# Attention's norm chains on ScalarE and GpSimd, and p's parts and the projection's first weight formed in the last slab in the values' buffers

## The chip, the cores and the metric

The kernel runs on one core of a Trainium2 chip. Its engines run side by side, each through its own list of instructions in order: TensorE (PE) multiplies matrices and transposes, VectorE (DVE), ScalarE (ACT) and GpSimd (POOL) work element by element, SyncE (SP) issues most transfers. What a program on one engine needs from another it waits for by semaphore. The metric is device time in microseconds (us) of one execution; runs of before took 1295.8 us in the median of three (1295.56 to 1299.09).

## What is computed

A trunk of two layers on one sequence of 512 tokens and 1024 features, in float32. Layer 0 mixes by a causal convolution, layer 1 by differential attention; each mixer is followed by a SwiGLU block and by a gated input embedding `p`. The change lies in layer 1, from attention to the gate:

```python
def diff_attention(x, w_qkv, q_g, k_g, ..., sub_g, w_o, rel_bias, lambda_init):
    q, k, v = jnp.split(x @ w_qkv, 3, axis=-1)          # 8 heads, two halves of 64 for q and k
    q = rms_norm(q.reshape(B, S, N_HEADS, 2, HEAD_DIM), q_g) * (HEAD_DIM ** -0.5)
    k = rms_norm(k.reshape(B, S, N_HEADS, 2, HEAD_DIM), k_g)
    ...
        logits = q_blk @ k + bias                        # causal, blocks of 128 queries
        probs = jax.nn.softmax(logits, axis=-1)
        w = probs[:, :, 0] - lam * probs[:, :, 1]        # the second half is taken off
        return w @ v
    o = rms_norm(o, sub_g) * (1.0 - lambda_init)         # per head, 128 features
    return o @ w_o

h = h + diff_attention(rms_norm(h, attn_norm_g), ...)
h = h + swiglu(rms_norm(h, ffn_norm_g), w_gate, w_up, w_down)
h = h + sigmoid(rms_norm(h, ple_norm_g) @ ple_w_gate) * (p @ ple_w_proj)
```

`rms_norm` divides by the root of the mean square plus an epsilon of 1e-6.

## The kernel before

**Tiling.** Features lie on the 128 partitions, tokens along the free axis: `h` is eight tiles of 128x512. Every product runs as three matmuls (`mm3`, lines 156 to 158), since each operand is held as a rounded high part and a remainder. `weight()` (line 136) makes the two parts of a 128x1024 block of weights: SP loads it into one of two raw buffers (`wraw`, line 145), ACT casts the high part (`whi`, line 149), DVE or POOL subtracts for the low part (`wlo`, line 151); `whi` and `wlo` have four buffers each. A raw buffer is free for the next load only once its low part is made.

**Order.** The program is written as one sequence; a scheduler then orders each engine's list by a simulated timeline, keeping dependencies. A tile is named by a tag with so many buffers, and a new tile of a tag waits until all readers of the old one in that buffer are done. So what the change moves is seen in the lists of the engines.

**Attention.** The loop over `QKV` (line 897) has six slabs of four weights: q and k of head pair 0, values of heads 0 to 3, pairs 1 and 2, values of heads 4 to 7, pair 3. Each slab runs over four blocks of 128 tokens (`tokens`, 24 matmuls a block). `values` leaves its two parts in the tiles B0 to B3 (heads 0 to 3) and B4 to B7. `unit` forms q and k of a pair: ACT copies and squares (lines 757, 760), DVE sums over 64 features (764) and adds the epsilon (235), POOL raises to the power -1/2 (237) and multiplies (767); `unit_end` transposes on PE (773) and writes the parts into the tiles C0 to C5 (two buffers each, so pair 3 takes pair 1's).

Between these matmuls stand the stages of the 32 pairs of head and query block: `stage_s` (logits 818 and 819 on PE, bias and minimum 821 and combining 830 on DVE, exponential 825 on ACT), `stage_t` (transposes 838, parts 840 and 841) and `stage_a` (product with the values 854 and 855, evacuation 861 and 862). After a head's last block `stage_a` normalises it: ACT squares all 512 columns (866), DVE sums (868), inverts the first softmax's sum (870), multiplies twice by it (871, 872) and adds the epsilon (235), POOL takes the power, DVE multiplies once more (874), POOL scales the head (876). `stage_o` transposes it (883) and splits it into the tiles A (180, 181).

**After the slabs.** `pfeatures` loads the two halves of p into raw buffers and splits them (lines 274, 275) into new tiles of the tags C0 and C1, whose next buffers are those of pair 2. `project` forms eight 128x512 products of p from two weights, with one step of the remaining attention stages before each. Then `linear` makes the attention's output product, eight outputs of 24 matmuls: the first two together, each head as it is ready, then one by one; `add_attn` adds each to `h` (951). PSUM has four accumulators of the tag `mm` for slabs, values, projections and outputs alike.

## Time and profile before

| | |
|---|---|
| median of three runs | 1295.8 us (1295.56 to 1299.09) |
| the profiled execution, its time | 1293.82 us |
| its span | 1292.0 us |
| instructions in the span | 15534 |

The profile is of one execution on the chip; times in it count from the start of the span, and the rest of that execution's time lies around it. A row of instructions names line, engine, operation, the tile written and those read, and the shape. Behind a bar stand busy time and the mean of one in nanoseconds. A table of windows gives for each stretch the busy time of each engine, its count of instructions, then the clock granted to PE and the share of the transfer engines. PE's matmuls are pipelined, so that one of 0.39 us in a row is followed by the next 0.23 us later.

### The profile page before, as it was taken

The page shows a single profiled execution, that of the slowest core. Times are in us where ns is not written, and L with a number is a line of the kernel's source. Part 1 is how long each engine was busy: PE and PEld are TensorE (multiplying, and loading weights), DVE is VectorE, ACT ScalarE, POOL GpSimd, SP SyncE. Part 2 cuts the span into 40 slices and gives each one's busy share as a digit, 9 for nine tenths or more (in the row PEclk, how much of TensorE's full clock was granted, in tenths as well). Part 3 has the DMA queues.
Part 4 walks back from the last instruction along what each step waited for, and adds up shares of the span by engine and source line. Part 5 has one row for each costly group of instructions (what it writes and reads, how often), then busy time and mean ns, then how long its engine had stood idle before and what let it go on. Part 6 is the DMA issues. An engine that isn't in the chain of part 4 may idle for free.

```text
span 1292.0 us, 15534 instructions
## 1 busy us (share of the span) xinstructions
PE 1269.5 (98%) x5960; PEld 1053.6 (82%) x5960; DVE 736.9 (57%) x1143; ACT 521.6 (40%) x826; POOL 236.8 (18%) x199
## 2 busy tenths in 40 slices
PE   9999999999999999999999997989999999999998
PEld 8888788888888888888888886878888888888887
DVE  4897866543344334457678988845443344334445
ACT  5742554332222223345566766634222233222332
POOL 1753432000000000042526534121000000000020
PEclk9999999999999999999999998999999999999999
DMA  7555223333333322233222223123333333332231
GB/s 273 192 177 181 80 76 104 98 98 98 98 98 99 97 86 95 82 117 98 88 90 74 74 66 83 57 76 103 99 98 94 89 97 96 98 98 90 90 115 66
DMA packets 46839, 131.98 MB, mean 102 GB/s; under 512 B 5379, under 2 KB 9987, under 8 KB 46764
## 3 DMA queue, kind: packets, MB, share of 16 engines
q1 hardware_dynamic: 44640, 127.55, 31.0%
q10 hardware_dynamic: 2124, 3.43, 1.0%
q8 instruction: 47, 0.77, 0.2%
q14 instruction: 28, 0.23, 0.1%
HBM read 126.75 MB, written 4.21 MB: 101 GB/s over the span
## 4 chain that ended last, share of the span: by engine, by line
PE 88%; DVE 6%; DMA 3%; issue 2%; ACT 1%; POOL 0%; SPq 0%; DVEq 0%; POOLq 0%; ACTq 0%
PE mm L156 28%; PE mm L157 27%; PE mm L158 27%; DVE sc L419 2%; DVE wlo L151 1%; PE tp L173 1%; PE mm L854 1%; DMA wraw<-in_wts 1%; DMA po<-big 1%; PE sc L818 1%; PE sc L368 1%; PE sc L819 1%; PE tp L838 1%; PE tp L773 0%; DMA h<-in_xT 0%
## 5 line engine op out<-in xcount | busy, mean ns | idle before, releaser
L149 ACT CAST whi<-wraw 128x1024 fp32r<-128x1024 f32 (+2 forms) x213 | 217.6, 1026 | 554.6 <-PE mm L158 364.1
L156 PE MATMUL mm<-A,wlo 128*128 128x512 f32 (+1 forms) x1096 | 427.9, 390 | 4.5 <-DVE wlo L151 3.0
L157 PE MATMUL mm<-A,whi 128*128 128x512 f32 (+1 forms) x1096 | 425.7, 389 | 0.0
L158 PE MATMUL mm<-A,whi 128*128 128x512 f32 (+1 forms) x1096 | 421.8, 389 | 0.0
L151 DVE TENSOR_TENSOR wlo<-wraw,whi 128x1024 fp32r<-128x1024 f32 (+2 forms) x209 | 259.4, 1245 | 84.8 <-ACT whi L149 84.7
L156 PEld LDWEIGHTS mm<-A,wlo 128*128 128x128 f32 x1096 | 206.0, 188 | 48.5 <-DVE wlo L151 3.5
L157 PEld LDWEIGHTS mm<-A,whi 128*128 128x128 f32 x1096 | 206.0, 188 | 42.8 <-issue 1.2
L158 PEld LDWEIGHTS mm<-A,whi 128*128 128x128 f32 x1096 | 205.4, 188 | 42.3 <-issue 0.5
L204 POOL TENSOR_TENSOR acc<-acc,wk 128x512 f32<-128x512 f32 x35 | 58.2, 1662 | 772.3 <-issue 660.1
L156 PE MATMUL mm<-B,wlo 128*128 128x512 f32 x352 | 137.8, 391 | 0.0
L157 PE MATMUL mm<-B,whi 128*128 128x512 f32 x352 | 137.4, 390 | 0.0
L158 PE MATMUL mm<-B,whi 128*128 128x512 f32 x352 | 137.4, 390 | 0.0
L635 DVE TENSOR_TENSOR h<-mm,h 128x512 f32<-128x512 f32 x48 | 33.0, 691 | 122.6 <-PE mm L158 122.5
L627 DVE TENSOR_TENSOR big<-mm,rb 128x512 f32<-128x512 f32 x44 | 30.4, 691 | 126.4 <-PE mm L158 126.4
L625 DVE TENSOR_TENSOR big<-mm,rb 128x512 f32<-128x512 f32 x44 | 30.4, 691 | 99.8 <-PE mm L158 93.0
L158 PEld LDWEIGHTS mm<-B,whi 128*128 128x128 f32 x352 | 66.1, 188 | 14.6
L157 PEld LDWEIGHTS mm<-B,whi 128*128 128x128 f32 x352 | 66.1, 188 | 14.3
L156 PEld LDWEIGHTS mm<-B,wlo 128*128 128x128 f32 x352 | 66.0, 188 | 14.2
L156 PE MATMUL mm<-whi,A 128*128 128x512 f32 x192 | 75.9, 396 | 0.0
L157 PE MATMUL mm<-whi,A 128*128 128x512 f32 x192 | 75.5, 393 | 0.0
L158 PE MATMUL mm<-wlo,A 128*128 128x512 f32 x192 | 74.7, 396 | 0.0
L237 POOL TENSOR_TENSOR r<-v,mhalf 128x8 f32<-128x8 f32 (+1 forms) x31 | 45.8, 1477 | 144.3 <-DVE v L235 135.8
(203 smaller groups left out, 1397.4 us busy)
## 6 DMA issues: line engine op xcount, KB each, us to landing
wraw<-in_wts SPq DMA_DIRECT2D x193, 512.0 KB, 3.5
wraw<-in_wts SPq DMA_DIRECT2D x16, 384.0 KB, 3.0
D<-in_diag SPq DMA_DIRECT2D x22, 256.0 KB, 4.3
C<-in_diag SPq DMA_DIRECT2D x16, 256.0 KB, 4.8
h<-in_xT SPq DMA_DIRECT2D x8, 256.0 KB, 5.4
bias<-scr ACTq DMA_DIRECT2D x8, 256.0 KB, 3.5
out_t<-h SPq DMA_DIRECT2D x7, 256.0 KB, 2.0
wraw<-in_wts SPq DMA_DIRECT2D x4, 256.0 KB, 5.0
```

The lines of the kernel that those rows point to most:

```text
L149: A.copy(hi[:, cut], raw[:, cut])
L151: eng.tensor_tensor(lo[:, cut], raw[:, cut], f(hi[:, cut]), ALU.subtract)
L156: T.matmul(acc, al, bh, start=first, stop=False)
L157: T.matmul(acc, ah, bh, start=False, stop=False)
L158: return T.matmul(acc, ah, bl, start=False, stop=last)
L173: r = T.matmul(t[:, cut], src[:, cut], ones, start=first and b == 0, stop=last and b == 3)
L204: self.last = self.eng.tensor_tensor(self.acc, self.acc, sq, ALU.add)
L237: last_pow[0] = G.tensor_tensor(r[:, :n], v[:, :n], mhalf[:, :n], ALU.pow)
L419: last_v_tap[0] = V.scalar_tensor_tensor(sum_, tap(j), wt(c, j), sum_, ALU.mult, ALU.add)
L625: V.tensor_tensor(tg, pg, rb, ALU.mult)
L627: V.tensor_tensor(tu, pu, rb, ALU.mult)
L635: V.tensor_tensor(h[m], acc, h[m], ALU.add)
```

## The change

1. In `unit` and in `stage_a` the norm no longer divides by the number of features. The sum of squares gets 64 or 128 times epsilon added and is raised to the power on POOL (two instructions on the same small tile); the constant factors are folded into the gains of k and of the sub-norm, so q's scale falls away.
2. In `stage_a` ACT squares each of the four blocks of 128 columns with a sum as accumulator, and the softmax's sum enters squared, as a factor of the epsilon. The six DVE instructions of a head's norm fall away; ACT has five small ones in place of one wide, POOL one more.
3. `pfeatures` is called behind the second token block of the last slab, into the tiles B0 and B1, and the projection's first weight behind the third, into B2 and B3. These held the values of heads 0 to 3.
4. The eight projections go to tiles C2 to C5 alone.
5. Weights 4 and 5 of the attention's output product get their parts in B0 to B3.

The diff, with all that the steps speak of:

```diff
--- before.py
+++ after.py
@@ -119,8 +119,10 @@
     make_identity(nc, ident)
     ones_r = sb([P, P], "ones", 1, F32R)
     ones = f(ones_r)
-    mhalf = sb([P, 2 * P], "mhalf", 1)[:, :8]
+    powers = sb([P, 2 * P], "mhalf", 1)
+    mhalf, meps = powers[:, :8], powers[:, 8:16]
     V.memset(mhalf, -0.5)
+    V.memset(meps, DH * EPS)
     t = wk()[:, 0:P]
     V.memset(t, 1.0)
     V.tensor_copy(ones_r, t)
@@ -134,12 +136,12 @@
     wnext = [0]
     loaded = [None]
 
-    def weight(n=1024, pieces=1, between=(), eng=V, after=(None, None), home=None):
+    def weight(n=1024, pieces=1, between=(), eng=V, after=(None, None), home=None, parts=None, bufs=1):
         i = wnext[0]
         wnext[0] += 1
         raw = sb([P, 1024], *(home or ("wraw", 2)))
-        hi = sb([P, 1024], "whi", 4, F32R)
-        lo = sb([P, 1024], "wlo", 4, F32R)
+        hi = sb([P, 1024], *((parts[0], bufs) if parts else ("whi", 4)), F32R)
+        lo = sb([P, 1024], *((parts[1], bufs) if parts else ("wlo", 4)), F32R)
         for k in range(pieces):
             cut = slice(k * n // pieces, (k + 1) * n // pieces)
             loaded[0] = nc.sync.dma_start(raw[:, cut], wts[i, :, cut])
@@ -578,13 +580,13 @@
             if c == 3:
                 third = lo, hi
 
-    def linear(n_in, src, consume, group0=1, before=None, after=None, split={}, home=None):
+    def linear(n_in, src, consume, group0=1, before=None, after=None, split={}, home=None, parts={}):
 
 
         m = 0
         while m < NC:
             g = group0 if m == 0 else 1
-            ws = [weight(n_in * P, after=split.get(m + i, (None, None)), home=home if m + i == 2 else None) for i in range(g)]
+            ws = [weight(n_in * P, after=split.get(m + i, (None, None)), home=home if m + i == 2 else None, parts=parts.get(m + i)) for i in range(g)]
             accs = [mm() for _ in range(g)]
             for k in range(n_in):
                 if before:
@@ -702,9 +704,10 @@
     V.tensor_tensor(lam[:, 2:3], lam[:, 1:2], lam[:, 0:1], ALU.subtract)
     V.tensor_scalar(lam[:, 3:4], lam[:, 2:3], -LAMBDA_INIT, None, ALU.add)
     mlam = lam[:, 3:4]
+
     gains = lam[:, 4:6]
-    V.tensor_scalar(gains[:, 0:1], col("q_g"), float(DH) ** -0.5, None, ALU.mult)
-    V.tensor_scalar(gains[:, 1:2], col("sub_g"), 1.0 - LAMBDA_INIT, None, ALU.mult)
+    V.tensor_scalar(gains[:, 0:1], col("k_g"), float(DH) ** 0.5, None, ALU.mult)
+    V.tensor_scalar(gains[:, 1:2], col("sub_g"), (1.0 - LAMBDA_INIT) * math.sqrt(P), None, ALU.mult)
 
     u = norm.u
     rcol = [None]
@@ -760,9 +763,11 @@
             A.activation(sq, acc, AF.Square, scale=r)
         else:
             G.tensor_tensor(sq, q, q, ALU.mult)
-        ss = sb([P, P // 2], "v8", 2)[:, :8]
-        V.tensor_reduce(out=ss, in_=sq.rearrange("p (g d) -> p g d", g=8), op=ALU.add, axis=AX.X)
-        rs = rsqrt_cols(ss, 8, 1.0 / DH)
+
+        rs = sb([P, P // 2], "r8", 2)[:, :8]
+        V.tensor_reduce(out=rs, in_=sq.rearrange("p (g d) -> p g d", g=8), op=ALU.add, axis=AX.X)
+        G.tensor_tensor(rs, rs, meps, ALU.add)
+        G.tensor_tensor(rs, rs, mhalf, ALU.pow)
         q3 = q.rearrange("p (g d) -> p g d", g=8)
         G.tensor_tensor(q3, q3, rs.unsqueeze(2).to_broadcast([P, 8, DH]), ALU.mult)
         return pair, tb, q
@@ -775,7 +780,7 @@
         cut = slice(tb * P, (tb + 1) * P)
         qs, ks, kl = qk[pair][0:2], qk[pair][2:4], qk[pair][4:6]
 
-        qg, kg = gains[:, 0:1], col("k_g")
+        qg, kg = col("q_g"), gains[:, 0:1]
         for c in range(2):
             own, other = HALVES[c], HALVES[1 - c]
             A.activation(qs[c][own, :, cut], t4[own, :, 0], AF.Copy, scale=qg[own])
@@ -862,16 +867,17 @@
             V.tensor_tensor(half, t4[:, :, 0], half, ALU.add)
         if qb == 3:
             o_ = osb[hd]
+
+            rs = sb([P, P // 2], "r8", 2)[:, :8]
+            e0 = sb([P, 4], "r0", 1)
+            A.activation(e0, stats[hd][:, :, 2], AF.Square, scale=math.sqrt(P * EPS))
             sq = wk()
-            A.activation(sq, o_, AF.Square)
-            ss = sb([P, P // 2], "v8", 2)[:, :8]
-            V.tensor_reduce(out=ss[:, 0:4], in_=sq.rearrange("p (g d) -> p g d", g=4), op=ALU.add, axis=AX.X)
-            r0 = sb([P, 4], "r0", 1)
-            V.reciprocal(r0, stats[hd][:, :, 2])
-            V.tensor_tensor(ss[:, 0:4], ss[:, 0:4], r0, ALU.mult)
-            V.tensor_tensor(ss[:, 0:4], ss[:, 0:4], r0, ALU.mult)
-            rs = rsqrt_cols(ss[:, 0:4], 4, 1.0 / P)
-            V.tensor_tensor(rs, rs, r0, ALU.mult)
+            for k in range(4):
+                cut = slice(k * P, (k + 1) * P)
+                A.activation(sq[:, cut], o_[:, cut], AF.Square, accum_out=rs[:, k : k + 1])
+            G.tensor_tensor(rs[:, 0:4], rs[:, 0:4], e0, ALU.add)
+            G.tensor_tensor(rs[:, 0:4], rs[:, 0:4], mhalf[:, 0:4], ALU.pow)
+            rs = rs[:, 0:4]
             o3 = o_.rearrange("p (g d) -> p g d", g=4)
             G.tensor_tensor(o3, o3, rs.unsqueeze(2).to_broadcast([P, 4, P]), ALU.mult)
 
@@ -911,7 +917,13 @@
                 values(at, ws, tb, between)
             else:
                 waiting = unit(at, ws, tb, between)
+
+            if (what, at, tb) == ("q", 3, 1):
+                ph = pfeatures(1, [both(sb([P, 2, S], t, 1, F32R)) for t in ("B0", "B1")])
+            elif (what, at, tb) == ("q", 3, 2):
+                pw = [weight(parts=("B2", "B3"))]
     unit_end(*waiting)
+    pw.append(weight())
 
 
     done = [0]
@@ -926,20 +938,12 @@
             stage_o(done[0])
             done[0] += 1
 
-    ph = pfeatures(1, [both(sb([P, 2, S], t, 2, F32R)) for t in ("C0", "C1")])
     pp = []
     for m in range(NC):
-        if m % 4 == 0:
-            w = weight()
+        if m % 2 == 0:
+            o2 = sb([P, 2, S], f"C{m // 2 + 2}", 2)
         step()
-        if m < 2:
-            o = sb([P, S], f"D{m + 2}", 1)
-        elif m % 2 == 0:
-            o2 = sb([P, 2, S], f"C{m // 2 + 1}", 2)
-            o = o2[:, 0]
-        else:
-            o = o2[:, 1]
-        pp.append(project(ph, m, w, o, step))
+        pp.append(project(ph, m, pw[m // 4], o2[:, m % 2], step))
 
     def heads_until(k):
         while done[0] <= k:
@@ -951,7 +955,7 @@
         V.tensor_tensor(h[m], acc, h[m], ALU.add)
         norm.chunk(m)
 
-    linear(NC, ot, add_attn, 2, heads_until, step)
+    linear(NC, ot, add_attn, 2, heads_until, step, parts={4: ("B0", "B1"), 5: ("B2", "B3")})
     n2 = Norm("ple_g1")
     ffn(norm, n2)
```

How the lists of the engines move, at three places. In the rows, numbers behind a tile's tag tell tiles apart; line numbers of the changed kernel are two to six higher than before.

PE, at the end of the last slab, behind the products of head 4's last block. Before, directly behind the logits of head 5's last block: `sc_6561`, `sc_6599` and `sc_6637` are logits of head 6, `tp_6428` the transposes of the slab's last token block, `tp_6483` head 0's (`stage_o`), `mm_6520` the first projection.

```order
L818 MATMUL sc_6561<-C_1154_6147,C_1152_6145 128x128
L819 MATMUL sc_6561<-C_1156_6149,C_1152_6145 128x128
L818 MATMUL sc_6599<-C_1154_6147,C_1152_6145 128x256
L819 MATMUL sc_6599<-C_1156_6149,C_1152_6145 128x256
L818 MATMUL sc_6561<-C_1155_6148,C_1153_6146 128x128
L819 MATMUL sc_6561<-C_1157_6150,C_1153_6146 128x128
L818 MATMUL sc_6637<-C_1154_6147,C_1152_6145 128x384
L819 MATMUL sc_6637<-C_1156_6149,C_1152_6145 128x384
L773 MATMUL tp_6428<-ident_65,big_6417 128x128 x4
L883 MATMUL tp_6483<-ident_65,D_918_5089 128x128 x4
L156 MATMUL mm_6520<-C_1210_6443,wlo_6455 128x512
L157 MATMUL mm_6520<-C_1210_6443,whi_6454 128x512
```

Now, 15 rows behind those logits, among which the first two projections stand (`mm_6554` is the third projection, on p's parts in B tiles, `sc_6558` and `sc_6520` are logits of head 6, `tp_6401` the transposes of the last token block, `tp_6444` head 0's):

```order
L158 MATMUL mm_6554<-B_1151_6259,B_1162_6320 128x512
L159 MATMUL mm_6554<-B_1151_6259,B_1161_6319 128x512
L160 MATMUL mm_6554<-B_1151_6259,B_1161_6319 128x512
L158 MATMUL mm_6554<-B_1152_6260,B_1162_6320 128x512
L159 MATMUL mm_6554<-B_1152_6260,B_1161_6319 128x512
L160 MATMUL mm_6554<-B_1152_6260,B_1161_6319 128x512
L823 MATMUL sc_6558<-C_1122_6112,C_1120_6110 128x256
L824 MATMUL sc_6558<-C_1124_6114,C_1120_6110 128x256
L823 MATMUL sc_6520<-C_1123_6113,C_1121_6111 128x128
L824 MATMUL sc_6520<-C_1125_6115,C_1121_6111 128x128
L778 MATMUL tp_6401<-ident_65,big_6392 128x128 x4
L889 MATMUL tp_6444<-ident_65,D_908_5080 128x128 x4
```

The first projection stood behind head 0's transposes; now the third one ends ahead of them, and only three matmuls of the first stand ahead of head 5's last logits.

ACT, p's casts. Before, right behind the q and k of the slab's last token block (`C_1211` is the second of p's high parts, `big_6527` and `rb_6533` are the exponentials of head 5's last block, `wk_6469` the squares of head 4, `whi_6454` the projection's first weight):

```order
L274 CAST C_1211_6444<-wraw_6449 128x512
L781 ACTIVATE C_1152_6145<-tp_6399,lam_4521 64x2x128
L782 ACTIVATE C_1154_6147<-tp_6399,vec_63 64x2x128
L781 ACTIVATE C_1153_6146<-tp_6399,lam_4521 64x2x128
L782 ACTIVATE C_1155_6148<-tp_6399,vec_63 64x2x128
L825 ACTIVATE big_6527,st_6201<-big_6527,st_6201 128x512
L866 ACTIVATE wk_6469<-D_1174_6234 128x512
L825 ACTIVATE rb_6533,st_6201<-rb_6533,st_6201 128x512
L692 DMA bias_6739<-scr 128x512
L825 ACTIVATE big_6564,st_6560<-big_6564,st_6560 128x128
L149 CAST whi_6454<-wraw_6453 128x1024
```

Now (`whi_6105` is the last weight of the last slab, `B_1151` and `B_1152` p's high parts, `B_1161` the projection's first weight, `big_6143` q and k of the slab's first token block, `wk_6041` the squares of head 3):

```order
L830 ACTIVATE acc_6010,st_5913<-acc_6010,st_5913 128x384
L276 CAST B_1151_6259<-wraw_6261 128x512
L866 COPY D_1080_5946<-mm_5991 128x256
L845 CAST wth_6073<-tp_6070 128x256
L830 ACTIVATE big_6055,st_5913<-big_6055,st_5913 128x512
L877 ACTIVATE wk_6041,r_1097_6038<-D_1080_5946 128x128 x2
L276 CAST B_1152_6260<-wraw_6265 128x512
L873 ACTIVATE r_1182_6434<-st_5913 128x4
L830 ACTIVATE rb_6061,st_5913<-rb_6061,st_5913 128x512
L694 DMA bias_6517<-scr 128x512
L151 CAST B_1161_6319<-wraw_6318 128x1024
L760 ACTIVATE big_6143<-mm_6118,rcol_4586 128x512
```

p's casts and the weight's cast stood behind the last token block of the slab; now they stand ahead of the first one.

ACT, at the end of attention. Before, `A_1361` is head 7's split, `whi_7130` and `whi_7169` are the fifth and sixth weight of the output product, `acc_7041` and `wk_7048` squares of the finished `h`:

```order
L180 ACTIVATE A_1358_7002<-tp_6997,lam_4521 128x512
L861 COPY D_1347_6945<-mm_6963 128x256
L866 ACTIVATE wk_6983<-D_1347_6945 128x512
L180 ACTIVATE A_1361_7014<-tp_7009,lam_4521 128x512
L149 CAST whi_7130<-wraw_7129 128x1024
L149 CAST whi_7169<-wraw_7168 128x1024
L200 ACTIVATE acc_7041<-h_7_86 128x512
L203 ACTIVATE wk_7048<-h_8_87 128x512
```

Now (`B_1335` and `B_1342` are those two weights, `whi_7035` is the fourth, `rb_6852` head 7's last exponential, `A_1273` head 5's split):

```order
L151 CAST B_1335_7074<-wraw_7073 128x1024
L288 COPY C_1257_6718<-mm_6764 128x512
L151 CAST whi_7035<-wraw_7034 128x1024
L877 ACTIVATE wk_6832,r_1286_6829<-D_1258_6723 128x128 x2
L830 ACTIVATE rb_6852,st_6691<-rb_6852,st_6691 128x512
L182 ACTIVATE A_1273_6788<-tp_6783,lam_4522 128x512
L845 CAST wth_6797<-tp_6795 128x128
L866 COPY D_1258_6723<-mm_6757 128x256
L151 CAST B_1342_7113<-wraw_7112 128x1024
```

The two casts stood behind head 7's split and now stand ahead of the exponential and the squares that lead to it.

## The prediction, made before the result was known

> **What bounds the kernel now.** First the page's span and the busy time of each engine.
>
> ```profile
> span 1292.0 us, 15534 instructions
> ## 1 busy us (share of the span) xinstructions
> PE 1269.5 (98%) x5960; PEld 1053.6 (82%) x5960; DVE 736.9 (57%) x1143; ACT 521.6 (40%) x826; POOL 236.8 (18%) x199
> ```
>
> TensorE (PE) is busy for 1269.5 of 1292.0 us. An edit to another engine can save only where PE waits, or where its clock is down: 22.5 us of idle time in the whole kernel. So I next cut the span at the places where the stages of attention change, and read the busy time by stretch.
>
> ```profile
> core 0: us, PE busy (x) PEld busy (x) DVE busy (x) ACT busy (x) POOL busy (x), PEclk, DMA share, GB/s
> ...
> 620.00:745.65 125.65, 124.98 (x640) 104.30 (x638) 95.99 (x236) 81.72 (x181) 61.94 (x60) 1.00 0.24 80
> 745.65:786.20 40.55, 39.17 (x214) 33.56 (x214) 33.46 (x100) 26.68 (x65) 16.90 (x17) 1.00 0.16 53
> 786.20:806.80 20.60, 13.40 (x59) 10.56 (x58) 17.91 (x44) 14.57 (x33) 7.00 (x8) 0.75 0.46 120
> ...
> 827.70:850.50 22.80, 22.80 (x126) 19.39 (x125) 9.07 (x26) 5.96 (x13) 4.09 (x4) 1.00 0.09 24
> 850.50:857.90 7.40, 3.59 (x18) 2.52 (x16) 4.42 (x7) 4.36 (x7) 0.55 (x1) 1.00 0.00 0
> 857.90:1292.00 434.10, 429.64 (x1916) 355.22 (x1916) 201.19 (x242) 130.85 (x164) 25.70 (x16) 1.00 0.31 97
> ```
>
> Two stretches carry the loss that the change can reach. From 786.2 us (the last logits of head 5) to 806.8, PE is busy for 13.40 of 20.60 us, and at a granted clock of 0.75. From 850.5 (the transposes of head 7) to 857.9, when the fifth output of the attention's last product begins, it is busy for 3.59 of 7.40. Ahead of 786 the idle time is 0.67 and 1.38 us; 4.46 us lie behind 857.9, in code that the change leaves alone.
>
> What ends the first wait stands in the rows of the raw weight buffers from 787 to 800 us.
>
> ```profile
> L145 SPq DMA_DIRECT2D wraw<-in_wts x3: 327/328/328, 790.1 to 798.7; - x3
> L274 ACT CAST C<-wraw x2: 638/640/642, 787.0 to 787.7; 128x512 fp32r<-128x512 f32 x2
> L275 DVE TENSOR_TENSOR C<-wraw,C x2: 690/777/864, 789.2 to 790.2; 128x512 fp32r<-128x512 f32 x2
> L149 ACT CAST whi<-wraw x2: 1028/1036/1044, 796.4 to 797.7; 128x1024 fp32r<-128x1024 f32 x2
> L151 DVE TENSOR_TENSOR wlo<-wraw,whi x2: 1222/1224/1226, 797.5 to 799.0; 128x1024 fp32r<-128x1024 f32 x2
> its engine sat idle before it (us, times) until:
>   DMA wraw<-in_wts: 4.0, 1
> ...
> DMA to landing us min/median/max: 3.4/6.3/6.6
> ```
>
> p's two halves are cast at 787.0, as soon as head 5's logits have given up the C buffers. Only then is their raw buffer free for the next weight, which is issued at 790.1. It lands 6.3 us later; ScalarE (ACT) stands 4.0 us at its cast, with an exponential queued behind it, VectorE (DVE) makes the low part at 797.5, and PE gets its first filling product at 798.7. The filler comes just after the hole that it could have filled.
>
> **The first stretch, part by part.** The stretch that moves as one is 786.2 to 827.7 us, from the logits of head 5 to the last logits of head 7.
>
> ```profile
> 786.20:827.70 41.50, 32.74 (x172) 27.02 (x172) 37.61 (x106) 32.71 (x79) 9.05 (x10) 0.88 0.35 96
> ```
>
> In 41.5 us DVE is busy for 37.6 and ACT for 32.7. PE's work at full clock is at most 32.74 x 0.88 = 28.8 us. So DVE, with 3.9 us of waiting, sets the pace. The change takes from it by these rows of the same stretch:
>
> ```profile
> L151 DVE TENSOR_TENSOR wlo<-wraw,whi 128x1024 fp32r<-128x1024 f32 x6 | 7.3, 1224 | 2.6 <-ACT whi L149 2.6
> ...
> L868 DVE TENSOR_REDUCE v<-wk 128x4 f32<-128x512 f32 x2 | 1.4, 686 | 0.2 <-ACT wk L866 0.2
> ...
> L874 DVE TENSOR_TENSOR r<-r,r 128x4 f32<-128x4 f32 x2 | 0.5, 256 | 0.0
> L870 DVE RECIPROCAL r<-st 128x4 f32<-128x4 f32 x2 | 0.4, 177 | 0.0
> L235 DVE TENSOR_SCALAR v<-v 128x4 f32<-128x4 f32 x2 | 0.3, 167 | 0.0
> L872 DVE TENSOR_TENSOR v<-v,r 128x4 f32<-128x4 f32 x2 | 0.3, 162 | 0.0
> ```
>
> Two heads' norm chains leave DVE: 1.4 + 0.5 + 0.4 + 0.3 + twice 0.3 (two equal multiplications) = 3.2 us. p's low parts go to the last slab: 2 x 0.78 = 1.6. The order shows three low weight parts in place of six behind head 5's logits: 3 x 1.22 = 3.7. DVE loses 8.5 us: 37.6 - 8.5 = 29.1.
>
> ACT is paid with part of it:
>
> ```profile
> L149 ACT CAST whi<-wraw 128x1024 fp32r<-128x1024 f32 x6 | 6.3, 1054 | 5.9 <-DMA wraw<-in_wts 5.9
> ...
> L825 ACT ACTIVATION_READ_ACCUMULATOR big<-big,st 128x1 f32 x9 | 1.8, 198 | 0.0
> ...
> L866 ACT ACTIVATE wk<-D 128x512 f32<-128x512 f32 x2 | 1.2, 622 | 0.2 <-DVE D L862 0.2
> ...
> L825 ACT ACTIVATE big<-big,st 128x128 f32<-128x128 f32 x2 | 0.8, 406 | 0.0
> ```
>
> It loses three weight casts (3.2), p's two casts (1.3) and two wide squares (1.2), together 5.7. It gains eight squares of 128x128 with an accumulator. No such square stands in the trace; the nearest row is the exponential of that size with its read, 0.41 + 0.20 less some overlap, so 0.53 each (bounds 0.16, a quarter of the wide square, and 0.60). That is 4.2, with 0.4 for two tiny squares (a read's 0.2 each): 32.7 - 5.7 + 4.6 = 31.6 (bounds 28.7 and 32.2).
>
> In PE's list 15 matmuls of p's projection now stand between head 5's logits and head 0's transposes. They are the hole's filling. What is late next is the chain itself: with DVE at 29.1, ACT at 31.6 and PE at 28.1 (three matmuls went ahead of 786.2) the three are nearly even, and ACT, with in-order waits on the other two, is the longest. Before, the longest engine was busy for 37.6 of 41.5; with half of its 3.9 us of waits left I take 31.6 + 1.9 = 33.5, that is **-8.0 us**. Bounds: 28.1 (PE alone), -13.4, and 41.5, nothing gained.
>
> [...]
>
> **Ahead of 786.2.** The three matmuls are a delay of 3 x 0.23 = **+0.7 us** (0.23 from one start to the next, 853.57 to 853.80 in the rows of the tail below). SP's list of transfers has the same rows in the same order, so p's loads overtake nothing; the freed raw buffer only lets the later loads go earlier. p's casts and the first weight's cast are now queued on ACT inside the last slab, p's first half only three instructions behind the cast that frees its raw buffer, and the exponentials of head 5 and the slab's first q and k wait behind them. PE has cover there: the slab's four blocks of 24 matmuls (4 x 24 x 0.23 = 22 us) need only their own weights. Without it one transfer costs up to 6.3 less what ACT has ahead. The idle 0.67 and 1.38 us can shrink as DVE has less to do. I take 0 for waits here, bounds -2 and +4.
>
> GpSimd (POOL) gets 24 additions of an epsilon, 128x8 or 128x4. No row has that operation; the bounds are the power of the same tile and a cast:
>
> ```profile
> L237 POOL TENSOR_TENSOR r<-v,mhalf 128x8 f32<-128x8 f32 x16 | 28.5, 1779 | 30.7 <-DVE v L235 28.1 <-ACT wk L866 2.2
> ...
> L786 POOL CAST C<-C 64x256 fp32r<-64x256 f32 x32 | 13.4, 417 | 21.6 <-ACT C L782 20.3
> ```
>
> I take the cast's 0.4, the nearest in being plain arithmetic, and keep 0 and 1.8. POOL has 61.94 + 16.90 busy of 166.2 us ahead of 786.2, so 20 additions (8 to 36 us) fit. In each chain the addition takes the place of a DVE step of 0.16 to 0.22 and its queue: nothing. The other edits (gains folded into k and the sub-norm, one more memset) keep the number of instructions on the path.
>
> **The tail.** After head 7 the fifth weight was late:
>
> ```profile
> 854.23 2.48 DVE L951 TENSOR_TENSOR h<-mm,h 128x512 f32<-128x512 f32 x4 [1.64 <-PE mm L158]
> 856.63 3.45 DVE L151 TENSOR_TENSOR wlo<-wraw,whi 128x1024 fp32r<-128x1024 f32 x2
> ...
> 853.57 0.39 PE L157 MATMUL mm<-A,whi 128*128 128x512 f32 x1
> 853.80 1.07 PE L158 MATMUL mm<-A,whi 128*128 128x512 f32 x4
> 857.90 0.50 PE L156 MATMUL mm<-A,wlo 128*128 128x512 f32 x1 [3.03 <-DVE wlo L151]
> ```
>
> PE waited 3.03 us for a low part that stood behind four additions to h. Weights 4 and 5 now get p's B buffers, and the order has their casts ahead of head 7's split. What is late next is an accumulator: all four are taken until the first addition to h frees one. That begins at 854.23 and takes some 0.7 us (2.48 for four), while PE ends its four matmuls at 853.80 + 1.07 = 854.87, so about 0.1 us of waiting is left: 3.03 - 0.1, **-2.9 us**. The split of head 7 that PE also waits for stays. From 827.7 to 850.5 PE is full, and its list is the same: 0.
>
> **Sum.** -8.0 + 0.7 + 0 - 2.9 = -10.2 us. The profiled execution took 1293.8 us around its span of 1292.0; it becomes 1283.6. The median of the runs is 1295.8, 2.0 above it, so I forecast **1285.6 us**. About 0.3% (3.9 us) is what a measurement can tell from no change, so "same" is 1291.9 to 1299.7.
>
> **The rivals.** *The hole is filled whole.* If ACT may lag behind PE as far as its buffers allow, PE alone sets the stretch: -13.4, and -2 ahead of it: 1295.8 - 13.4 + 0.7 - 2.0 - 2.9 = 1278. For it: ACT had 5.9 us of waits for transfers there, most of which go. Against it: three engines evenly loaded and working in turn.
>
> *The hole only moves.* Filling used before head 0's transposes is missing after them, where head 6's logits each wait for DVE. If ACT's longer queue gives back all of the first term, only the tail is left: 1295.8 + 0.7 - 2.9 = 1293.6. For it: the order has no filling between head 0's transposes and the fourth projection.
>
> *GpSimd's additions hold up DVE.* At 1.8 us each, and DVE standing still meanwhile, the five in the stretch (one unit's, three or four heads') take 9 us: DVE 38.1, no gain there, and five before it in the last slab cost PE what DVE has too little slack for (33.46 of 40.55 busy): about 2 us; 1295.6. Against it: beside the power from 704.20 to 705.84 DVE's rows have their usual length:
>
> ```profile
> 704.20 1.64 POOL L237 TENSOR_TENSOR r<-v,mhalf 128x8 f32<-128x8 f32 x1 [4.03 <-DVE v L235]
> 704.38 0.08 DVE L821 DVE_READ_ACCUMULATOR2_ANT st<- 128x1 f32 x1
> 704.38 0.67 DVE L764 TENSOR_REDUCE v<-wk 128x8 f32<-128x512 f32 x1
> ```
>
> [...]
>
> *Slower: ACT stands in its queue for p.* In the last slab ACT now meets, one behind the other, p's first half, the projection's first weight and the next weights, each loaded only when the one before has been split. If each costs the 6.3 us of the row above and PE's blocks don't cover it (they need ACT to empty their accumulators), three of them are +18.9: 1285.6 + 18.9 = 1304.5. It decides from 14.1 us of uncovered waits on (10.2 + 3.9). Against it: 22 us of matmuls as cover.
>
> **How the numbers follow.** Forecast 0.65 (1280 to 1291), whole filling 0.12, the hole moves 0.11, GpSimd 0.05, slower 0.07. Faster by over 0.3%: 0.65 + 0.12 = 0.77, within: 0.11 + 0.05 = 0.16, slower 0.07. The range leaves out the slow case, GpSimd's and the far end of the first: 1279 to 1294.
>
> **What would show it.** Right: p's casts before 780 us, no wait of ACT for a weight over 2 us behind head 5's logits, projection matmuls ahead of head 0's transposes, 33 to 34 us from head 5's last logits to head 7's, clock over 0.9 there, and the fifth output's first matmul within 0.5 us of the fourth's end. Wrong: accumulating squares well over 0.53 us, additions on GpSimd near 1.8, or PE waiting in the last slab.

## The result, and the profile after

| | before | after |
|---|---|---|
| median of six runs each | 1297.3 us (1295.6 to 1302.2) | 1286.9 us (1284.3 to 1288.3) |
| ratio, 95% interval | | 0.9917 [0.9902, 0.9932] |
| profiled execution, its time | 1293.8 us | 1287.5 us |

The change makes the kernel faster by 0.8%, 10.4 us by the medians. The predicted 1285.6 us lies 1.3 below the median. The two profiled executions differ by 6.3 us only, and in them one term of the sum is wrong by half, so the agreement has to be taken apart. First the page of after:

```profile
span 1285.7 us, 15538 instructions
## 1 busy us (share of the span) xinstructions
PE 1269.5 (99%) x5960; PEld 1054.8 (82%) x5960; DVE 723.5 (56%) x1080; ACT 527.9 (41%) x890; POOL 241.5 (19%) x223
```

The table of windows for after, by stage; behind the times of the engines stand the granted clock and the share of the transfer engines. Head 5's last logits now start at 787.11, the second half of head 7's at 823.48, head 7's transposes at 847.13, the fifth output at 851.63.

```profile
core 0: us, PE busy (x) PEld busy (x) DVE busy (x) ACT busy (x) POOL busy (x), PEclk, DMA share, GB/s
...
746.20:787.10 40.90, 40.90 (x223) 35.05 (x222) 34.03 (x84) 31.28 (x80) 17.16 (x20) 1.00 0.31 97
787.10:794.00 6.90, 6.30 (x36) 5.24 (x34) 6.65 (x16) 6.66 (x17) 3.68 (x5) 1.00 0.52 174
794.00:800.00 6.00, 2.26 (x11) 1.61 (x12) 5.62 (x15) 5.53 (x21) 3.47 (x5) 0.89 0.33 108
800.00:810.00 10.00, 8.95 (x37) 7.33 (x36) 8.50 (x29) 6.28 (x16) 0.00 (x0) 0.55 0.01 2
810.00:823.50 13.50, 13.50 (x82) 11.91 (x81) 9.11 (x31) 11.14 (x37) 2.25 (x3) 1.00 0.01 2
787.10:823.50 36.40, 31.01 (x163) 26.10 (x162) 29.88 (x89) 29.61 (x89) 9.40 (x13) 0.86 0.16 52
823.50:847.13 23.63, 23.62 (x131) 20.21 (x129) 9.17 (x17) 9.52 (x31) 4.95 (x6) 1.00 0.20 67
847.13:851.63 4.50, 3.62 (x18) 2.53 (x16) 1.50 (x3) 1.44 (x2) 0.00 (x0) 1.00 0.00 0
```

The same stretch of before, cut at PE's rows (the prediction's 827.70 was DVE's end):

```profile
786.21:826.57 40.36, 31.60 (x168) 26.07 (x167) 36.53 (x105) 32.68 (x79) 9.05 (x10) 0.87 0.36 99
```

PE is full up to 793.4, where before the hole had begun at 787.9. From 794 it is busy for 2.26 of 6 us, and from 800 to 810 for 8.95 us, but at a clock of 0.55. The stretch is 36.4 us long, 4.0 less than before. The hole has moved, and the loss of clock with it. PE's rows there (start, duration; in brackets the wait and what ended it):

```profile
792.78 0.62 PE L778 MATMUL tp<-ident,big 128*128 128x128 f32 x4
794.14 0.63 PE L889 MATMUL tp<-ident,D 128*128 128x128 f32 x4 [0.74 <-DVE C L796]
795.73 0.41 PE L823 MATMUL sc<-C,C 128*128 128x384 f32 x1 [0.96 <-DVE st L826]
...
797.77 0.41 PE L823 MATMUL sc<-C,C 128*128 128x384 f32 x1 [1.22 <-DVE st L826]
798.02 0.34 PE L824 MATMUL sc<-C,C 128*128 128x384 f32 x1
799.78 1.94 PE L889 MATMUL tp<-ident,D 128*128 128x128 f32 x8 [1.42 <-DVE C L796]
```

All four waits end with DVE, for which the windows have 6.65 + 5.62 = 12.27 of 12.9 us from 787.1 to 800. No piece is longer than 1.42 us.

Where the time went, from head to tail (differences of the rows' starts; the first unit's transposes, row 2574 of PE's list in both kernels, stand at 637.59 and 640.15):

| stretch | before | after | change | forecast |
|---|---|---|---|---|
| to the first unit's transposes | 637.59 | 640.15 | +2.6 | 0 |
| to head 5's last logits | 148.62 | 146.96 | -1.7 | +0.7 |
| to head 7's last logits | 40.36 | 36.37 | -4.0 | -8.0 |
| to head 7's transposes | 23.91 | 23.65 | -0.3 | 0 |
| to the fifth output | 7.42 | 4.50 | -2.9 | -2.9 |
| rest of the span | 434.1 | 434.1 | 0.0 | 0 |

The first row is not the change. PE's idle time in the first 240 us was 3.42 us in the profile of before and 5.44 in that of after; over the fourteen profiles of this study it ran from 3.4 to 7.0 us, with no order by kernel, and before's is the least. So the profile on which the sum was built was an early starter by some 2 us. Attention itself, from the first unit's transposes to the fifth output, took 220.31 and 211.48 us: -8.8. The rest of the 10.4, some 1.6 us, stays open. Before was profiled once, and in a quick execution: its mean granted clock was 0.995. Of the 60 later executions of before on record, the ten with 0.995 took 1295.5 us on average, the other fifty (0.991 to 0.994) 1297.9. So a typical execution of before may lose more to the clock than the table shows; that the 1.6 us lie in this stretch is not shown.

The window of the first 240 us of before (240 less the first busy time is PE's idle time):

```profile
0.00:240.00 240.00, 236.58 (x1209) 198.07 (x1210) 174.32 (x216) 120.47 (x172) 93.06 (x75) 1.00 0.46 152
```

The same of after:

```profile
0.00:240.00 240.00, 234.56 (x1198) 196.05 (x1199) 173.43 (x216) 120.20 (x171) 93.18 (x75) 1.00 0.46 150
```

### The profile page after: what moved, and what is told of

It reads as the page before. It is cut to its first block, busy times and chain, and to the rows that moved or that the text cites. A ratio compares the mean times of both kernels' runs of the same rounds, so it can differ in the third digit from the quotient of the medians.

```text
span 1285.7 us, 15538 instructions
## 1 busy us (share of the span) xinstructions
PE 1269.5 (99%) x5960; PEld 1054.8 (82%) x5960; DVE 723.5 (56%) x1080; ACT 527.9 (41%) x890; POOL 241.5 (19%) x223
## 4 chain that ended last, share of the span: by engine, by line
PE 91%; DVE 4%; DMA 3%; issue 1%; ACT 0%; SPq 0%; POOL 0%; DVEq 0%; ACTq 0%
PE mm L158 28%; PE mm L159 28%; PE mm L160 28%; DVE sc L421 2%; PE mm L859 1%; DMA po<-big 1%; PE tp L175 1%; PE sc L824 1%; DMA wraw<-in_wts 1%; PE sc L823 1%; PE tp L843 1%; DVE wlo L153 1%; PE sc L370 1%; PE tp L778 1%; PE mm L860 0%
## 5 line engine op out<-in xcount | busy, mean ns | idle before, releaser
L151 ACT CAST whi<-wraw 128x1024 fp32r<-128x1024 f32 (+2 forms) x210 | 214.3, 1026 | 546.2 <-PE mm L160 360.8
L158 PE MATMUL mm<-A,wlo 128*128 128x512 f32 (+1 forms) x1080 | 421.3, 390 | 1.7 <-ACT A L182 1.7
L159 PE MATMUL mm<-A,whi 128*128 128x512 f32 (+1 forms) x1080 | 419.3, 389 | 0.0
L160 PE MATMUL mm<-A,whi 128*128 128x512 f32 (+1 forms) x1080 | 415.8, 389 | 0.0
L153 DVE TENSOR_TENSOR wlo<-wraw,whi 128x1024 fp32r<-128x1024 f32 (+2 forms) x206 | 256.3, 1248 | 79.9 <-ACT whi L151 78.3
L158 PEld LDWEIGHTS mm<-A,wlo 128*128 128x128 f32 x1080 | 203.0, 188 | 44.4 <-ACT A L182 2.2
L159 PEld LDWEIGHTS mm<-A,whi 128*128 128x128 f32 x1080 | 203.0, 188 | 42.0 <-issue 1.2
L160 PEld LDWEIGHTS mm<-A,whi 128*128 128x128 f32 x1080 | 202.7, 188 | 41.7 <-issue 0.5
L158 PE MATMUL mm<-B,wlo 128*128 128x512 f32 x360 | 140.9, 391 | 0.0
L159 PE MATMUL mm<-B,whi 128*128 128x512 f32 x360 | 140.6, 390 | 0.0
L160 PE MATMUL mm<-B,whi 128*128 128x512 f32 x360 | 140.6, 390 | 0.0
L160 PEld LDWEIGHTS mm<-B,whi 128*128 128x128 f32 x360 | 67.6, 188 | 14.9
L159 PEld LDWEIGHTS mm<-B,whi 128*128 128x128 f32 x360 | 67.6, 188 | 14.6
L409 POOL TENSOR_TENSOR wk<-wk,C 128x512 f32<-128x512 f32 x35 | 51.2, 1465 | 23.7 <-ACT C L408 18.8
```

The lines of the kernel that those rows point to most:

```text
L151: A.copy(hi[:, cut], raw[:, cut])
L153: eng.tensor_tensor(lo[:, cut], raw[:, cut], f(hi[:, cut]), ALU.subtract)
L158: T.matmul(acc, al, bh, start=first, stop=False)
L159: T.matmul(acc, ah, bh, start=False, stop=False)
L160: return T.matmul(acc, ah, bl, start=False, stop=last)
L409: G.tensor_tensor(pacc, pacc, pr, ALU.add)
```

## The experiments

### One part alone

The change falls into three parts: the norm chains, the move of p, and the tail (weights 4 and 5 in p's buffers). Three kernels have one part each, one has the two others without the tail.

```diff
+ linear(NC, ot, add_attn, 2, heads_until, step, parts={4: ("B0", "B1"), 5: ("B2", "B3")})   # before + this: tail alone
- linear(NC, ot, add_attn, 2, heads_until, step, parts={4: ("B0", "B1"), 5: ("B2", "B3")})   # after - this: no tail
```

The tail alone also takes over the argument `parts` of `weight` and `linear`. The kernel with the norm chains has the edits of the change to `mhalf`, `gains`, `unit` and `stage_a` alone; the one with p has those behind the `QKV` loop and in the projection.

> The kernel before with one part of the change alone: weights 4 and 5 of the attention's last product get p's buffers B0 to B3. Theory (the tail is a term by itself): the fifth output's first matmul starts within 0.5 us of the fourth output's end, the 3.03 us wait for the low part is gone, from head 7's transposes to that matmul it takes 4.5 us where it took 7.42, and the time falls by 2.9 us. Rival (another wait takes its place, the additions to h free the accumulators too late): the distance stays above 6.5 us and the time falls by less than 1 us.

> The changed kernel with weights 4 and 5 of the attention's last product in the ordinary weight buffers again. Theory: the wait of about 3 us for the fifth weight's low part comes back behind head 7's transposes, everything ahead of it stays as in the changed kernel (36.4 us from head 5's last logits to head 7's, clock near 0.55 in the 10 us behind head 0's transposes), and the time is 2.9 us above the changed kernel, 7 to 8 below the kernel before. Rival (the early forming of weights 4 and 5 costs ScalarE and VectorE time in the stretch ahead): the stretch becomes shorter by over 1 us and the time is less than 1.5 above the changed kernel.

> The kernel before with the norm chains of the change alone (units and heads on ScalarE and GpSimd; p, its parts and its first weight stay where they were). Theory (VectorE sets the pace of the stretch and is late ahead of it): VectorE loses 3.2 us in the stretch from head 5's last logits to head 7's, the 2.0 us of idle time ahead of 786 us go, the hole behind head 5's logits stays because the late weight fills it as before, and the time falls by 3 to 5 us. Rival (the hole is set by p's late casts and the weight behind them, VectorE's relief only gives longer waits): the stretch keeps its 40.4 us to within 0.7, only the 2.0 us ahead of it may go, and the time falls by 0 to 2 us.

> The kernel before with the move of p alone (p's parts and the projection's first weight formed in the last slab in B0 to B3, the outputs in C; norm chains as before, weights 4 and 5 in the ordinary buffers). Theory (the filler fills the first hole and the loss moves behind head 0's transposes): VectorE loses 1.6 + 3.7 us of 37.6, the stretch from head 5's last logits to head 7's falls from 40.4 to between 36.5 and 39 us, PE idles about 4 us in pieces behind head 0's transposes and its clock falls there below 0.7; the time falls by 1.5 to 4 us. Rival (the order alone makes the whole gain of the stretch, the norm chains nothing): the stretch is 36.4 us as in the changed kernel and the time falls by 4 to 7 us; or the added work in the last slab costs PE over 1 us of waits ahead of head 5's logits, where the changed kernel has none, and the gain is under 1 us.

| kernel | median, ratio to before | to head 5 | head 5 to 7 | to head 7's transposes | tail | clock halved for |
|---|---|---|---|---|---|---|
| before | 1297.6 | 148.6 | 40.4 | 23.9 | 7.42 | 10.2 us |
| tail alone | 1294.9, 0.9982 [0.9974, 0.9990] | 148.6 | 44.7 | 21.9 | 4.49 | 13.7 us |
| norm chains alone | 1297.8, 1.0004 [0.9993, 1.0015] | 146.2 | 45.2 | 22.5 | 7.40 | 10.2 + 6.8 us |
| p alone | 1296.4, 0.9994 [0.9986, 1.0003] | 149.5 | 39.0 | 24.0 | 7.43 | 3.4 + 3.4 us |
| norm chains and p | 1289.6, 0.9934 [0.9921, 0.9946] | 147.0 | 35.2 | 23.4 | 7.40 | 6.8 us |

(Stretches and clock are from one profile each; the last column counts the stretch from head 5's logits to head 7's transposes. Where the scheduler has put head 7's logits earlier or later in PE's list, the two stretches around them are to be added.)

**The tail** is a term by itself: 7.42 becomes 4.49 us, and 4.50 becomes 7.40 without it; by the medians it is worth 2.6 us alone and 2.7 to 3.0 against three series of the changed kernel (1286.9, 1286.5, 1286.5). The theory of both expectations holds. In the one profile of the tail alone the gain does not show in the total: from head 5's logits to head 7's transposes it takes 66.6 us instead of 64.3, with 13.7 us of half clock instead of 10.2. Where the stretch ahead came out 1.1 us shorter without the tail, its clock was halved for one piece less, of which below.

**The other two parts give nothing alone (+0.2 and -1.1 us, both intervals take in zero), and 8.0 us together.** Neither theory had that: 3 to 5 and 1.5 to 4 us were expected, and of the rivals only the bounds on the time fit (0 to 2 us, and under 1 us to within its noise). The norm chains alone do what was expected ahead of head 5's logits: the 2.0 us of waiting go. But PE then reaches the hole 2.4 us earlier, and p's late casts still hold up the raw buffers. ScalarE's rows of that kernel:

```profile
799.09 1.05 ACT L151 CAST whi<-wraw 128x1024 fp32r<-128x1024 f32 x1 [1.85 <-DMA wraw<-in_wts]
802.85 1.04 ACT L151 CAST whi<-wraw 128x1024 fp32r<-128x1024 f32 x1 [2.71 <-DMA wraw<-in_wts]
```

And PE's row behind them:

```profile
805.77 0.47 PE L821 MATMUL sc<-C,C 128*128 128x512 f32 x1 [2.67 <-DVE st L824]
```

Head 6's logits stand behind a low part on DVE (at 803.92), that behind a cast on ACT, and that behind a transfer. From head 5's logits to head 7's transposes it takes 67.7 us instead of 64.3. The loss of clock is not that of one profile alone: the mean granted clock is 0.992 in seven of the eleven executions of this kernel and 0.993 in four, and below 0.993 in only two of before's 60. With p alone the transfers are in time, but DVE still carries the chains; a window of that kernel:

```profile
793.00:800.20 7.20, 3.65 (x18) 3.01 (x18) 7.03 (x18) 6.04 (x14) 3.12 (x4) 1.00 0.58 159
```

And PE's row at its end:

```profile
800.24 0.33 PE L818 MATMUL sc<-C,C 128*128 128x128 f32 x1 [3.22 <-DVE st L821]
```

DVE is busy for 7.03 of 7.20 us, and PE waits 3.22 for it. (This profile is no typical one: its mean clock is 0.997, that of the ten other executions 0.993 to 0.995, like before's. The two short pieces of half clock in the table are therefore not the rule for this kernel.) So the hole has two limits, late transfers and a full DVE. Each part lifts one and leaves the other, and the gain comes only when both are gone.

### The same kernel again

The granted clock in these profiles is 1.00 or 0.50, and the halved pieces last 3.41, 6.83, 10.24 or 13.65 us. In all fourteen traces the times from one change of the clock to the next, between its first rise and its drop at the program's end, are whole multiples of 3.413 us, to within 2 ns: the full clock ahead of after's drop lasted 232 of them, in the second and third profile 231 and 232. So the changes lie on a grid, and the grid lies differently against the program in each execution. The changed kernel was profiled twice more.

> The changed kernel once more. What differs between executions of the same instructions? Theory (the clock is judged on a grid of about 3.4 us that does not start with the program, so the same waits fall differently into it): the idle pieces between 790 and 806 us are the same to within 0.3 us in sum (5.4 us), but the stretch of halved clock behind them can be another multiple of 3.4 us (10.2 us in the first profile), and the time from head 5's last logits to head 7's moves with half of it. Also the first 640 us come out about 2.3 us shorter or longer according to a wait of the convolution between 120 and 160 us. Rival (the dip follows from the waits alone): the dip is 10.2 us again and the stretch 36.4 us to within 0.4. Median 1286 to 1288.5 by both.

> The changed kernel a third time, beside the two kernels with the filler moved. Theory: a dip of a multiple of 3.4 us, of at least 6.8, and a stretch of 35 to 37 us from head 5's last logits to head 7's; median 1286 to 1288. Rival (the dips of 10.2 and 13.9 us were luck of the grid): a dip of 3.4 us or none, stretch under 35 us.

Medians 1286.5 and 1286.5 us (0.9917 both times). The windows of the stretch and of its halved piece, second profile:

```profile
784.24:821.05 36.81, 31.95 (x163) 26.71 (x161) 29.86 (x89) 29.75 (x88) 9.40 (x13) 0.81 0.16 51
793.40:807.00 13.60, 10.45 (x39) 8.16 (x38) 11.83 (x36) 9.41 (x26) 2.39 (x4) 0.50 0.14 39
```

Third profile:

```profile
787.20:824.75 37.55, 32.50 (x162) 27.13 (x161) 29.86 (x89) 29.65 (x88) 9.39 (x13) 0.82 0.16 50
798.00:811.50 13.50, 11.38 (x40) 8.97 (x41) 11.70 (x34) 8.94 (x29) 0.84 (x3) 0.50 0.03 12
```

The same instructions, with 5.4, 4.9 and 5.1 us of idle time in the stretch, get 10.2, 13.7 and 13.7 us of half clock: the theory's other multiple is there. The idle time does not agree to the 0.3 us that were expected, and 37.6 lies above the 35 to 37 of the third expectation. And the stretch did not move by half of it (36.4, 36.8, 37.6); that part of the slow time is covered by waits for DVE is likely, but not shown. In the 3.41 us ahead of the drop PE idles for 2.00, 1.70 and 2.16 us (50 to 63%), in pieces of 0.4 to 1.2 us. That window in the first profile:

```profile
795.30:798.71 3.41, 1.41 (x6) 0.94 (x6) 3.13 (x12) 3.36 (x11) 3.13 (x5) 1.00 0.47 154
```

In the second:

```profile
789.95:793.35 3.40, 1.70 (x13) 1.28 (x12) 3.27 (x10) 3.38 (x13) 1.20 (x3) 1.00 0.44 176
```

In the third:

```profile
794.45:797.86 3.41, 1.25 (x8) 0.85 (x7) 3.13 (x11) 3.36 (x13) 2.48 (x3) 1.00 0.38 104
```

### A filler moved into the hole

If the share of idle time counts, not the length of a hole, fillers have to be spread. Two kernels move the third projection's six matmuls (1.4 us), which stood in the full stretch ahead of the hole, behind head 0's transposes, or three behind head 0's and three behind head 1's. Nothing else changes in what is computed.

```diff
-        pp.append(project(ph, m, pw[m // 4], o2[:, m % 2], step))
+        with tc.issue_after(last_o[HOLD[m]].ins) if m in HOLD else nullcontext():    # HOLD = {2: 0}
+            pp.append(project(ph, m, pw[m // 4], o2[:, m % 2], (lambda: None) if m in HOLD else step))
+        if m in HOLD:
+            step()
+            step()
```

(`last_o[hd]` is the last transpose of head `hd`; with halves, `project` holds its part k behind `last_o[hold[k]]`. There the fourth projection is named too, behind heads 1 and 2; in the trace its matmuls keep their place, at 807.3 us.)

> The changed kernel with one filler moved: the six matmuls of the third projection (1.4 us) are issued behind head 0's transposes instead of ahead of head 6's second logits. Theory A (the share of idle time in 3.4 us decides on the clock, and spreading the filler keeps each such piece over half busy): the dip of 10.2 us falls to 3.4 or nothing, the stretch from head 5's last logits to head 7's from 36.4 to 33 to 35 us, the time is 1.5 to 3.5 us below the changed kernel. Theory B (VectorE's chain alone sets this stretch, the clock only uses its slack): the stretch stays at 36 to 37 us whatever the dip does, and the time is within 1 us of the changed kernel. Rival C (the hole opens ahead of head 0's transposes instead): a dip of the same length, beginning 3 to 7 us earlier.

> The kernel with the third projection's six matmuls behind head 0's transposes once more, for a second profile and more times. Theory A: dip of 3.4 us or none, stretch 33 to 35 us, median 1 to 2.5 us below that of the changed kernel (1286.5 to 1286.9). Rival (luck of the grid): dip of 7 us or more, stretch over 35.5 us, median 1286 to 1287.5.

> The changed kernel with the third projection in two halves: three matmuls behind head 0's transposes and three behind head 1's (0.7 us each), where the run with all six behind head 0's left idle pieces of 1.34 us ahead of head 0's transposes and 0.96 us behind. Theory A (clock by the share of idle time in about 3.4 us): idle time stays near 4 us, as VectorE's chain sets it, the dip is 3.4 us or absent, the stretch from head 5's last logits to head 7's 33 to 34.5 us against 36.4 and 36.8 in the two profiles of the changed kernel, the time 1 to 3 us below it. Rival (the one short dip of the run before was luck of the grid): a dip of 7 us or more again, stretch over 35.5 us, time within 1 us of the changed kernel.

> The kernel with the third projection in two halves once more, since its first median (1284.6 us, four runs) stands 1.9 us below the changed kernel's (1286.5) with intervals that overlap. Theory A: median 1284 to 1286 us again, the stretch of halved clock 3.4 us or none, 33 to 35 us from head 5's last logits to head 7's. Rival (chance): median 1286 to 1287.5, a dip of 7 us or more.

The window of the halved piece, with six matmuls behind head 0's transposes:

```profile
794.20:797.60 3.40, 3.00 (x9) 2.57 (x10) 3.27 (x10) 3.35 (x13) 1.90 (x3) 0.50 0.33 77
```

With three and three:

```profile
798.35:801.76 3.41, 2.77 (x9) 2.46 (x10) 3.30 (x11) 1.87 (x6) 0.47 (x2) 0.50 0.10 40
```

| | median, ratio to before | head 5 to 7 | idle in it | clock halved for |
|---|---|---|---|---|
| after, three times | 1286.9, 1286.5, 1286.5; 0.9917 [0.990, 0.993] | 36.4, 36.8, 37.6 | 5.4, 4.9, 5.1 | 10.2, 13.7, 13.7 us |
| six behind head 0 | 1285.6, 0.9904 [0.9889, 0.9919] | 34.0 | 4.1 | 3.4 us |
| the same again | 1285.9, 0.9904 [0.9889, 0.9920] | 34.8 | 5.2 | 3.4 us |
| three and three | 1284.6, 0.9898 [0.9884, 0.9911] | 34.7 | 5.7 | 3.4 us |
| the same again | 1286.2, 0.9914 [0.9896, 0.9933] | 34.3 | 5.4 | 3.4 us |

Four profiles of four have one short piece of half clock there, against three of three with a long one, with 4.1 to 5.7 us of idle time where the changed kernel has 4.9 to 5.4. The drop itself came in all four. In the 3.41 us behind it PE is busy for 81 to 94%, against 42 to 68% in the three profiles of the changed kernel, and the clock comes back after this one piece. The stretch is 2.4 us shorter on average (34.5 against 36.9), so a chain of DVE alone (theory B) does not set it. Nor was it luck of the grid: the record has a mean granted clock for every execution, and it is 0.994 to 0.997 in the 17 of the changed kernel (mean 0.9949) and 0.995 to 1.000 in the 20 with the filler moved (mean 0.9981). The piece does not follow the longest wait either: the last kernel's longest is 3.04 us, after's 1.42. In the medians 0.3 to 2.3 us of this are seen, and each interval overlaps those of the changed kernel. Taken together, the 20 executions are 1.6 us quicker on average than the 17 (1285.3 against 1286.9; 95% interval by resampling 0.6 to 2.5 us). So the moved filler beats the changed kernel as well, though by little.

### Less work in the hole

Two more edits take work from DVE there: the outputs of heads 0 to 3 transposed one per step, and three low weight parts formed on GpSimd.

```diff
-        while done[0] < NH and (n - LA - 3) // 4 > done[0]:
+        if done[0] < NH and (n - LA - 3) // 4 > done[0]:
```

```diff
-    pw.append(weight())
+    pw.append(weight(eng=G))                       # and the last product's first two weights likewise
```

> The changed kernel with head 0 to 3's outputs transposed one per step of the work list, not all four as soon as the buffers allow. Each brings VectorE 0.75 us and ScalarE 0.69 us of splitting. Theory B (VectorE's work in the hole is the bound): 1 to 2 of these splits leave the hole of 794 to 800 us, the stretch becomes 0.7 to 2 us shorter. Theory A (the clock): idle time in the hole falls below half of 3.4 us and the dip shortens with it, the gain is up to 4 us. Rival (only their place changes): within 1 us of the changed kernel.

> The changed kernel with three low weight parts (the projection's second weight and the last product's first two) formed by GpSimd instead of VectorE: 3 x 1.22 us leave VectorE between 786 and 796 us, and GpSimd gets 3 x 2.4 us. Theory B (VectorE's 12.3 us in the 12.9 us from 787.1 to 800 make the hole): PE's idle time in the stretch falls from 5.4 to between 2 and 3 us, the dip goes or becomes 3.4 us, the stretch falls from 36.4 to between 32 and 34 us, and the time is 2 to 4 us below the changed kernel. Rival (GpSimd's own chain, the power and the multiplication of the last units, stands behind the parts): the last unit's transposes come 2 us or more later and PE waits for them, the time is 0 to 3 us above the changed kernel. Second rival (GpSimd's parts hold up VectorE's operations beside them): VectorE's rows beside the 2.4 us parts are longer than elsewhere by over 0.5 us each, and the gain is under 1 us.

One per step: 1287.8 us, 0.9921 [0.9907, 0.9934]; 5.4 us idle, 10.2 us of half clock, 61.1 us from head 5's logits to head 7's transposes where the changed kernel has 60.0, 60.5 and 61.2. The time is 0.9 to 1.3 us above that of the changed kernel, with overlapping intervals. No gain, so the rival is nearest: only the places change.

On GpSimd: 1287.9 us, 0.9924 [0.9911, 0.9936]; PE idles 6.8 us in the stretch, not 2 to 3. Both rivals show; the time is 1.0 to 1.4 us above the changed kernel's, with overlapping intervals. PE waits 1.26 us for a copy of k queued behind the parts on GpSimd, and an operation on DVE takes far longer beside it; the longest wait is one of 2.48 us for DVE. POOL's rows of that kernel:

```profile
787.91 2.39 POOL L153 TENSOR_TENSOR wlo<-wraw,whi 128x1024 fp32r<-128x1024 f32 x1
...
795.15 1.46 POOL L882 TENSOR_TENSOR D<-D,r 128x512 f32<-128x512 f32 x1
```

DVE's rows beside them:

```profile
788.64 1.68 DVE L834 SCALAR_TENSOR_TENSOR st<-st,lam 128x1 f32<-128x1 f32 x1
...
795.82 0.80 DVE L834 SCALAR_TENSOR_TENSOR st<-st,lam 128x1 f32<-128x1 f32 x1
```

An operation of DVE on 128x1, 0.22 us elsewhere, takes 1.68 and 0.80 us, and ends both times when GpSimd's does (790.32 and 790.30, 796.62 and 796.61).

## Why the prediction was right, and where it was not

**The tail, -2.9: right, to the step.** PE's rows of after:

```profile
850.46 1.07 PE L160 MATMUL mm<-A,whi 128*128 128x512 f32 x4
851.63 0.50 PE L158 MATMUL mm<-A,B 128*128 128x512 f32 x1
```

And DVE's addition to h:

```profile
850.88 2.48 DVE L955 TENSOR_TENSOR h<-mm,h 128x512 f32<-128x512 f32 x4 [1.65 <-PE mm L160]
```

The four matmuls end at 851.53 and the fifth output starts 0.1 us later, some 0.7 us into the first addition to h: the wait for an accumulator that was named as late next.

**Ahead of head 5's logits, +0.7: mis-sized, -1.7.** "I take 0 for waits here, bounds -2 and +4." The waits went, 2.05 us in before, which is the lower of the two bounds. The norm chains alone show the same (146.2 against 148.6), p alone does not (149.5): it is DVE's relief. The feared wait of ACT for p did not reach PE, which is full there; p's casts in the lines view of after:

```profile
L276 ACT CAST B<-wraw x2: 609/615/621, 762.4 to 764.8; 128x512 fp32r<-128x512 f32 x2
...
  DMA wraw<-in_pT: 1.4, 1
```

**The first stretch, -8.0: half of it, -4.0.** ACT lost more than was worked out (32.7 to 29.6 us, 3.1 against 1.1), DVE less (36.5 to 29.9, 6.6 against 8.5): the fourth low part in the stretch, that of the output product's weight 4 at 823.06 us, which the fifth edit brings forward, is missing from the count of three. But it lies behind the hole, DVE came out close to the 29.1 of the sum and ACT below the 31.6. So the step that failed is "Before, the longest engine was busy for 37.6 of 41.5; with half of its 3.9 us of waits left I take 31.6 + 1.9 = 33.5". That takes three engines' sums over the whole stretch. But DVE's work lies bunched: 12.27 of 12.9 us up to 800, 9.11 of 13.5 behind 810. In the first part it stays the bound, and PE, having used its filler before, idles. Of the signs that were named, those on p's casts, on ACT's waits, on the projection and on the fifth output came; the 33 to 34 us and the clock over 0.9 did not (36.4 us, 0.86).

The second failure is the clock. The sum sets PE's 28.1 us at full clock beside DVE and ACT, and "clock over 0.9 there" was one of the signs; that the clock stays up there is shown by no run, and the three profiles of the changed kernel have 10.2, 13.7 and 13.7 us of half clock in its place. The holes are shorter (1.42 us at most, 2.71 before) and the clock went to half for as long, 10.2 us. Before's own trace could have warned: in the 3.41 us ahead of its drop (at 791.94) PE was busy for 1.27 us, and the longest wait of its hole, 2.71 us, had just begun (0.30 us earlier).

```profile
788.53:791.94 3.41, 1.27 (x6) 0.80 (x6) 3.36 (x11) 3.36 (x10) 2.29 (x3) 1.00 0.28 20
```

And PE's row of before with that wait:

```profile
794.35 0.66 PE L818 MATMUL sc<-C,C 128*128 128x384 f32 x1 [2.71 <-DVE v L871]
```

The traces show pieces of half clock of 3.41, 6.83, 10.24 and 13.65 us, different ones for the same instructions, and no long wait ahead of those of the changed kernel: 50 to 63% of idle time, in pieces of 0.4 to 1.2 us, stood in the 3.41 us ahead of its three drops.

The moved filler parts the two failures: the forecast would have made the stretch 32.4 us (40.4 - 8.0), after's three profiles have 36.9 on average, and with one short piece of half clock it is 34.5. Of the 4.5 us missing, 2.4 go with the long halved pieces, and 2.1 stay, with one short halved piece and waits mostly for DVE. The size rests on before's one profile: by the medians the norm chains and p together are worth 8.0 us, which less the 1.7 ahead of the stretch would leave 6.3 for it. The shortfall is then between 1.7 and 4.0 us.

**The prices.** The lines view of after, for the accumulating square and its read, and for the two additions (min/median/max in ns):

```profile
L877 ACT ACTIVATE wk<-D x32: 293/306/327, 681.8 to 841.6; 128x128 f32<-128x128 f32 x32
L877 ACT ACTIVATION_READ_ACCUMULATOR wk<-D x32: 185/188/209, 682.0 to 841.8; 128x1 f32 x32
...
L769 POOL TENSOR_TENSOR r<-r,mhalf x16: 200/203/323, 633.5 to 789.0; 128x8 f32<-128x8 f32 x16
...
L878 POOL TENSOR_TENSOR r<-r,r x8: 200/203/651, 685.4 to 842.1; 128x4 f32<-128x4 f32 x8
```

0.49 us for square and read, that overlap to 0.3 from pair to pair (0.53 taken), 0.20 for an addition (0.4 taken, 1.8 as the rival had it): an addition is not priced like the power on the same tile.

**The rivals.** *Filled whole* and *slower* did not come. *Only moves* named the right place, "the order has no filling between head 0's transposes and the fourth projection", but "gives back all" was too much. *GpSimd holds up DVE* had a mechanism that exists: beside a low part of 2.39 us and a multiplication of 1.46 us on GpSimd the operation of DVE on 128x1 took 1.68 and 0.80 us in place of 0.22; at 0.2 us an addition there is little to hold up. But not every pair of operations conflicts: the reduction beside the power of 704.20, which the prediction held against this rival, kept its 0.67 us, and in the trace with the low parts on GpSimd an operation of DVE on two larger tiles (a SCALAR_TENSOR_TENSOR of L835, 790.36) kept its usual 0.75 us beside a power (790.27 to 791.90). What parts the two kinds was not tried.

**The sum** came out near in part by luck. In attention -1.7 and -4.0 stand for +0.7 and -8.0, together -8.8 in place of -10.2. Before's median of more runs is 1297.3 and not 1295.8, which should have put after at 1288.5 by the profiles; the 1.6 us that the medians show beyond them, and that stay open, brought it to 1286.9. So a shortfall in the stretch, a gain ahead of it that was put at nothing, and a start from two quick figures of before set each other off.

## What to carry to other kernels

Cut a stretch in short pieces before taking the longest engine's sum as its length: work that is bunched at one end keeps its hole, whatever the mean says (here DVE was busy for 29.88 of 36.4 us, but for 12.27 of the first 12.9). Spread filling matmuls over the waits rather than issuing them as early as they are ready: here 1.70 to 2.16 us of idle time in 3.41 us, in short pieces, stood ahead of 10.2 to 13.7 us of half clock, and with the filler moved the piece was 3.4 us in four profiles of four. Two limits on one hole are to be lifted together; either edit alone can measure as nothing (+0.2 and -1.1 us here, 8.0 together).
